# Hybrid block kernel: low-part weight pass moved to the front of each tile, and separate places for low parts

## The chip, the cores and the metric

The kernel runs on one core of a Trainium2 chip. The metric is device time in microseconds (us) of one execution. Before the change the median of three runs is 1329.59 us (1329.51 to 1330.32).

## The reference

Two layers of a hybrid block on 272 tokens (16 meta tokens and 256 of the sequence) of 1024 features. Each layer normalizes, projects the tokens into twelve groups of features, runs three token mixers (retention, HGRN2, differential attention), joins them by gates, projects back, and ends with a gated feed-forward part with a convolution over three tokens. All is float32. Cut to the products with weights, which take nearly all of the time:

```python
proj = (hn @ w_in).astype(F32)
...
y_b = jnp.einsum('blnc,ncd->blnd', branches, w_branch.astype(F32))
...
return y.astype(hn.dtype) @ w_out
...
u = jnp.where(valid[None, :, None], hn @ w_ffn_in, 0.0)
...
return (jax.nn.silu(gate) * val) @ w_ffn_out
```

## The kernel before

**Tiles and passes.** The weights are a stream of 128x128 tiles, 1616 for each layer, in the order in which they are used. A product is computed with features on partitions: a weight tile is the stationary operand, and one 128-feature slice (a "k tile") of the activations, 272 tokens wide, is the moving operand. Each operand is split into a high part, rounded to the float32r format, and a low part, the rest. Three float32r passes go into one PSUM accumulator: high weights with high activations (L868), high weights with low activations (L869), low weights with high activations (L870). Every pass is one LDWEIGHTS and one MATMUL, and TensorE loads the weights of a pass while the pass before still streams. Below, a "step" is the time from the start of one such MATMUL to the start of the next.

**Order.** `ORDER` and `_turns` (L87) list the products in pairs of output tiles. For a pair the order is k = 0 to 7, and for each k the two output tiles (f = 0, 1), so that of two neighbouring tiles every second one moves on to the next k. Only the first two pairs of layer 0 run together: there four tiles share each of the first four k, and every fourth moves on. The feed-forward input is `fi` with 22 pairs (j = 0 to 21) in each layer; its output `fo` has four pairs of 44 tiles in layer 0, and another form in layer 1 (`final`, L1346), where 512 columns of weights stream as the moving operand. In layer 1 most products run on 258 tokens alone (`t0` = `T0` = 14, the first 14 are not needed any more): the moving operand begins 56 bytes later. I call these "short"; the six groups in `FULL` and all of layer 0 have 272 ("full").

**Places of the weights.** Eight tiles arrive in one DMA (`wraw`, 512 KB, a "chunk"). ACT writes their high parts to `whi`, DVE the low parts to `wlo`, four buffers each (`_Weights.next`, L572). `_places` (L125) chooses where in its buffer a tile lies: `APART` and `BLOCK` say at which byte modulo 256 (`LINE`) it is to begin, and 64 is added for each k, as the k tiles of the activations, 1088 bytes long, each begin 64 bytes further modulo 256. High and low part of a tile have the same place. `_runs` (L150) joins tiles whose places follow one rule, so that one ACT and one DVE instruction cut them.

**Distances.** By the addresses in the built program the activations `xh`, `xl` begin at a multiple of 256 bytes and the weight buffers 64 bytes past one; the slots that `b0` to `b2`, `wo` and `fo` use begin at 64 too, which `BLOCK` makes up for. By "distance" I mean the byte address of the weights that are being loaded less that of the operand that streams meanwhile, modulo 256. In full products it is 64 as long as the next pass has the same k, and 128 where the next tile has the next k (L870 streams the high part of k while the high weights of k + 1 are loaded). In short products the two are 104 and 168. The last pair of `fo` in layer 0 has no place asked for (`None`): its tiles lie end to end, and the distance goes through 0, 192, 128 and 64.

**Queues.** All instructions are put in order by a list scheduler (`_Plan.order`) with a modelled cost for each. The cut of a chunk is keyed `LEAD` = 6 us ahead of its first use.

Of the kernel before, what the change touches and what calls it, by code (L numbers as in the profile page):

```python
# [11 lines left out]
F32 = mybir.dt.float32  # L12
F32R = mybir.dt.float32r
U8 = mybir.dt.uint8
AF = mybir.ActivationFunctionType
ALU = mybir.AluOpType
PSUM = bass.MemoryType.PSUM
ADD, SUB, MUL = ALU.add, ALU.subtract, ALU.mult

P = 128  # L20
# [16 lines left out]
CHUNK_TILES = 8  # L37
# [49 lines left out]
def _turns(li):  # L87

    pairs = [x for x in ORDER if x[0][0] not in MARKS]
    if li == DEPTH - 1:
        pairs = [x for x in pairs if x[0] != "fo"]
    groups = [[x] for x in pairs]
    if li == 0:
        groups[:2] = [pairs[:2]]
    turned = [[x] for n in (BASE, ("fi",)) for x in [x for x in pairs if x[0] in n][DEFER - 1 : DEFER]]
    out = []
    for group in groups:  # L100
        if group == [("fo", 3)]:
            out.append([("fo", 3, k, f) for f in range(2) for k in range(FK)])
        else:
            nk = _ktiles(group[0][0])
            out.append([x + (k, f) for k in range(nk // 2) for x in group for f in range(2)])
            out[-1] += [x + (k, f) for x in group for k in range(nk // 2, nk) for f in range(2)]
            if group in turned:
                out[-1] = out[-1][nk:] + out[-1][:nk]
    if li == DEPTH - 1:
        out.append([("fo", j, k, f) for k in range(FK) for j in range(KD // 2) for f in range(2)])  # L110
    return out
# [3 lines left out]


LINE = 256
APART = (0, 96)
BLOCK = 64
ROOM = CHUNK_TILES * P + 2 * LINE // 4  # L120
T0 = META - 2
FULL = ("rk", "rv", "hf", "hi", "dk", "dv")


def _places(depth=DEPTH):  # L125

    wants = []
    for li in range(depth):  # L130
        for name, j, k, _ in sum(_turns(li), []):
            if name == "fo" and (li == DEPTH - 1 or j == 3):
                wants.append(None)
                continue
            short = li == DEPTH - 1 and name not in FULL
            wants.append(APART[short] + BLOCK * (name[0] == "b" or name in ("wo", "fo")) + 64 * (k % 4))
    out = []
    for c in range(0, len(wants), CHUNK_TILES):
        at, places = 0, []
        for want in wants[c : c + CHUNK_TILES]:  # L140
            if want is not None:
                at += (want // 4 - at) % (LINE // 4)
            places.append(at)
            at += P
        assert at <= ROOM
        out.append(places)
    return out


def _runs(places):  # L150


    runs = []
    for i, at in enumerate(places):
        if runs and at == runs[-1][1] + runs[-1][2] * P:
            runs[-1][2] += 1
        else:
            runs.append([i, at, 1])
    out = []
    for i, at, n in runs:  # L160
        if out and out[-1][4] == n and (out[-1][3] == 1 or at == out[-1][1] + out[-1][2] * out[-1][3]):
            if out[-1][3] == 1:
                out[-1][2] = at - out[-1][1]
            out[-1][3] += 1
        else:
            out.append([i, at, 0, 1, n])
    return out


# [388 lines left out]
class _Weights:  # L558
# [6 lines left out]
        self.used = 0  # L565
        self.places = _places()

    def part(self, t, at, step, runs, n):

        return bass.AP(t.tensor, t.offset + at, [list(t.ap[0]), [max(step, 1), runs], [1, n * P]])  # L570

    def next(self):  # L572
        c, i = divmod(self.used, CHUNK_TILES)
        self.used += 1
        if i == 0:
            due = self.plan.key
            room = [P, ROOM]
            raw = self.plan.tile(self.pool, [P, CHUNK_TILES * P], F32, "wraw", 3, f"wraw{c}")
            hi = self.plan.tile(self.pool, room, F32R, "whi", 4, f"whi{c}")
            lo = self.plan.tile(self.pool, room, F32R, "wlo", 4, f"wlo{c}")  # L580
            self.plan.key = due - LEAD
            pieces = 1 if c > 1 else 2
            for p in range(pieces):
                n = CHUNK_TILES // pieces
                cols = slice(p * n * P, (p + 1) * n * P)
                self.sp.dma_start(raw[:, cols], self.w[c][:, cols])
                for first, at, step, runs, each in _runs(self.places[c][p * n : (p + 1) * n]):
                    src = raw[:, (p * n + first) * P : (p * n + first + runs * each) * P].rearrange("p (r x) -> p r x", r=runs)
                    self.act.activation(self.part(hi, at, step, runs, each), src, AF.Copy)
                    self.dve.tensor_tensor(out=self.part(lo, at, step, runs, each), in0=src, in1=self.part(hi, at, step, runs, each).bitcast(F32), op=SUB)  # L590
            self.plan.key = due
            self.cut = hi, lo
        hi, lo = self.cut
        at = self.places[c][i]
        return hi[:, at : at + P], lo[:, at : at + P]

    def chunk(self):

# [13 lines left out]
def _trace(ctx, tc, plan, a, depth, probe):  # L612
    nc = tc.nc
# [79 lines left out]
    inner = masks[:64, 2 * 64 :]  # L693
# [78 lines left out]
    class Norm:  # L772
# [42 lines left out]
        def next(self):  # L815

            self.pairs += 1
            if self.pairs != DEFER + 1:
                return
            self.folded = True  # L820
            ys = []
            for k in range(KD):
                plan.key = clock[0] - 12.0 + 0.3 * k
                if k % 4 == 0:
                    ys.append(slot4("y"))
                y = ys[-1][:, k % 4, :]
                pool.tensor_tensor(out=y, in0=h[:, k, :], in1=rstd, op=MUL)
                plan.key = clock[0] - 6.0 + 0.7 * k
                hi, lo = x_tile(k, True)
                act.activation(hi, y, AF.Identity, scale=self.g[:, k : k + 1])  # L830
                stt(lo, y, self.g[:, k : k + 1], hi.bitcast(F32), MUL, SUB)
# [13 lines left out]
    def products(xs, name, j, t0=0):  # L845

        if name in BASE or name == "fi":
            norm.next()
        if ahead:
            return ahead.pop()  # L850
        tiles = turns.pop(0)
        main = lambda: new(mp, [P, 2, 512], F32, "main", 2, "main")[:, :, t0:T]
        ps = {i: main() for i in sorted({x[1] for x in tiles})}
        to = {x: ps[x[0]][:, x[1], :] for x in {x[1::2] for x in tiles}}
        if (name, j) == ("fo", 3):

            to[j, 1] = main()[:, 1, :]
        cost = 3 * ((T - t0) / 2400 + 0.003)
        left = dict.fromkeys(to, _ktiles(name))
        for _, i, k, f in tiles:  # L860
            hi, lo = (x[:, t0:] for x in xs(k))
            begun = left[i, f] < _ktiles(name)
            left[i, f] -= 1
            plan.key = clock[0]
            wh, wl = weights.next()

            def run(o=to[i, f], wh=wh, wl=wl, hi=hi, lo=lo, first=not begun, last=left[i, f] == 0):
                nc.tensor.matmul(o, wh, hi, start=first, stop=False)  # L868
                nc.tensor.matmul(o, wh, lo, start=False, stop=False)  # L869
                nc.tensor.matmul(o, wl, hi, start=False, stop=last)  # L870

            plan.main.append(plan.add("pe", run, cost, [to[i, f]], [wh, wl, hi, lo]))
            clock[0] += cost
        plan.key = clock[0] - 1.0
        if (name, j) == ("fo", 3):
            return [to[j, f] for f in range(2)]
        ahead.extend(ps[i] for i in ps if i != j)
        return ps[j]
# [64 lines left out]
    for li in range(depth):  # L943
        last = li == depth - 1
# [457 lines left out]
        for name, j in ORDER:  # L1402
# [4 lines left out]
            elif name in ("+hga", "+hgb"):  # L1407
                b = "ab".index(name[3])
# [3 lines left out]
            elif name in ("+daa", "+dab"):  # L1412
                b = "ab".index(name[3])
# [7 lines left out]
            elif name[0] == "*":  # L1421
                plan.key = clock[0] - MARGIN
                n = name[1:]
                if n == "b2":
                    blocks = [st["da0"], st["da1"]]
                else:
                    t = st["rg" if n == "b0" else "hg"]
# [4 lines left out]
            two = slice(2 * (j % 2), 2 * (j % 2) + 2)  # L1432
            both = slice(2 * j, 2 * j + 2)
            if name in BASE:
                lo = 0 if name in FULL else t0
# [17 lines left out]
                elif name in ("dq", "dk"):  # L1453
                    t = block(f"{name}{j // 2}")
# [3 lines left out]
                elif name == "rv":  # L1458
# [3 lines left out]
                    src = values(ps, st["rvt"][j // 2], (j % 2) * 2 * P)  # L1462
# [4 lines left out]
                elif name in ("hi", "dv"):  # L1467
                    n = name[0] + "v"
                    b = j // 2
# [5 lines left out]
                    src = values(ps, st[f"{n}t{b}"], (j % 2) * 2 * P)  # L1475
# [6 lines left out]
                else:  # L1482
                    t = block(f"{name}{j // 2}")
# [21 lines left out]
            elif name == "wo":  # L1505
                hi, lo = st["yhi"], st["ylo"]
# [8 lines left out]
            elif name == "fi":  # L1515
# [8 lines left out]
                first = META if last else 0  # L1524
                c = temp2("two_b")
                for f in range(2):
# [4 lines left out]
                    for back in (1, 2):  # L1531
                        at = max(first, back)
                        stt(c[:, f, at:], u[:, f, at - back - t0 : T - back - t0], w(2 - back), c[:, f, at:], MUL, ADD)
                c = c[:, :, first:]
# [6 lines left out]
            else:  # L1541
                hi, lo = st["ghi"], st["glo"]
# [35 lines left out]
```

## Time and profile before

| | before |
|---|---|
| median of 3 runs | 1329.59 us |
| span of the profiled execution | 1327.6 us |
| TensorE busy (MATMUL) | 1317.0 us, 99% |
| LDWEIGHTS busy | 1288.8 us, 97% |
| DVE busy | 962.7 us, 73% |
| ACT busy | 816.7 us, 62% |
| DMA from HBM | 216.16 MB |

The span is that of one profiled execution from its first to its last instruction; its own time as a run is not listed apart, and the median lies 2.0 us above the span, for what is ahead of the first instruction and behind the last. MATMULs overlap in the records (each has some 290 ns, though one starts every 125 ns), so the busy share says only that TensorE is never without work; what a pass costs is read from the starts. In the timeline a row gives the start in us, the duration in us, the engine, the line, the operation, and output<-input; what stands in brackets is idle time ahead of it and what ended it.

### The profile page before, as it was taken

Reading aid. Unit: us, or ns where it says so; the run is one execution under the profiler, and the core shown is the slowest. Engines: PE = TensorE matmul, PEld = TensorE weight load, DVE = VectorE, ACT = ScalarE, POOL = GpSimd, SP = SyncE. Lnnn points to the kernel's source line nnn. Section 1 sums busy time; section 2 is a strip of 40 time slices with the busy share of each in tenths; the row PEclk is TensorE's granted clock in tenths of the full one; section 3 lists DMA queues with packets and bytes.
Section 4 is the critical chain, followed back from the end, with each engine's and each line's share of the span. In section 5 each row is a group of like instructions: output and inputs, shape, how many; then the busy total and the mean of one; then the engine's idle time right before and its main releaser. Section 6 shows DMA issues by size and latency. Waiting matters only on the chain.

```text
span 1327.6 us, 28926 instructions
## 1 busy us (share of the span) xinstructions
PE 1317.0 (99%) x11862; PEld 1288.8 (97%) x11862; DVE 962.7 (73%) x1630; ACT 816.7 (62%) x1374; POOL 83.6 (6%) x161
## 2 busy tenths in 40 slices
PE   9999999999999999999999999999999999999998
PEld 9999999999999999999999999999999999999986
DVE  7675777697586789886574757776985867898753
ACT  6747454756676567666456474557565775767643
POOL 5000000001010020000030000000011100200000
PEclk9999999999999999999999999999999999999999
DMA  7644543443534545555555445444445446465653
GB/s 272 195 146 155 170 150 128 143 143 129 188 131 158 177 157 176 187 168 186 175 175 181 155 159 161 160 140 143 143 149 175 142 162 199 135 208 189 201 182 109
DMA packets 60755, 219.07 MB, mean 165 GB/s; under 512 B 6864, under 2 KB 6992, under 8 KB 60624
## 3 DMA queue, kind: packets, MB, share of 16 engines
q1 hardware_dynamic: 60336, 216.71, 49.1%
q8 instruction: 93, 1.52, 0.5%
q10 hardware_dynamic: 288, 0.52, 0.1%
q14 instruction: 38, 0.31, 0.1%
HBM read 216.16 MB, written 1.05 MB: 164 GB/s over the span
## 4 chain that ended last, share of the span: by engine, by line
PE 95%; DVE 3%; issue 1%; DMA 0%; ACT 0%; SPq 0%; DVEq 0%
PE main L868 28%; PE main L870 27%; PE main L869 27%; PE fo L1380 2%; PE fo L1378 2%; PE fo L1379 2%; PE lev L1059 1%; DVE two_b L553 1%; PE ds L1243 1%; PE ms L553 1%; PE do L553 1%; DVE wlo L553 1%; PE ro L553 1%; PE ho L553 1%; PE vt L553 1%
## 5 line engine op out<-in xcount | busy, mean ns | idle before, releaser
L868 PE MATMUL main<-xh,whi 128*128 128x272 f32 (+1 forms) x2368 | 693.2, 293 | 0.2 <-ACT whi L553 0.2
L870 PE MATMUL main<-xh,wlo 128*128 128x272 f32 (+1 forms) x2368 | 680.5, 287 | 0.8 <-DVE wlo L553 0.7
L869 PE MATMUL main<-xl,whi 128*128 128x272 f32 (+1 forms) x2368 | 671.6, 284 | 1.6 <-DVE xl L553 1.5
L553 DVE TENSOR_TENSOR wlo<-wraw,whi 128x1024 fp32r<-128x1024 f32 (+1 forms) x408 | 497.1, 1223 | 200.9 <-ACT whi L553 199.8
L553 ACT ACTIVATE whi<-wraw 128x1024 fp32r<-128x1024 f32 (+1 forms) x408 | 426.6, 1048 | 229.5 <-PE main L869 162.2
L869 PEld LDWEIGHTS main<-xl,whi 128*128 128x128 f32 x2368 | 448.9, 190 | 2.5 <-DVE xl L553 2.1
L868 PEld LDWEIGHTS main<-xh,whi 128*128 128x128 f32 x2368 | 445.6, 188 | 2.5 <-issue 0.7
L870 PEld LDWEIGHTS main<-xh,wlo 128*128 128x128 f32 x2368 | 444.6, 188 | 2.2 <-DVE wlo L553 2.1
L553 DVE SCALAR_TENSOR_TENSOR two_b<-main,small,two_b 128x256 f32<-128x256 f32 (+2 forms) x144 | 65.3, 488 | 29.1 <-ACT two_b L553 27.4
L553 POOL TENSOR_TENSOR y<-h,rstd 128x272 f32<-128x272 f32 x32 | 34.6, 1114 | 316.7 <-ACT rstd L553 316.7
L553 ACT ACTIVATE two_b<-main,small 128x272 f32<-128x272 f32 (+1 forms) x72 | 37.3, 567 | 26.8 <-PE main L870 26.6
L870 PE MATMUL main<-ghi,wlo 128*128 128x272 f32 x176 | 51.0, 290 | 0.0
L868 PE MATMUL main<-ghi,whi 128*128 128x272 f32 x176 | 50.9, 289 | 0.0
L869 PE MATMUL main<-glo,whi 128*128 128x272 f32 x176 | 50.2, 285 | 0.0
L553 ACT ACTIVATE vsrc<-main 128x544 f32<-128x544 f32 x24 | 15.0, 626 | 39.4 <-PE main L870 39.2
L868 PE MATMUL main<-b0hi,whi 128*128 128x272 f32 (+1 forms) x128 | 38.1, 298 | 0.0
L868 PE MATMUL main<-b1hi,whi 128*128 128x272 f32 (+1 forms) x128 | 38.1, 298 | 0.0
L870 PE MATMUL main<-yhi,wlo 128*128 128x272 f32 (+1 forms) x128 | 36.7, 286 | 0.0
L870 PE MATMUL main<-b2hi,wlo 128*128 128x272 f32 (+1 forms) x128 | 36.6, 286 | 0.0
L870 PE MATMUL main<-b1hi,wlo 128*128 128x272 f32 (+1 forms) x128 | 36.6, 286 | 0.0
L870 PE MATMUL main<-b0hi,wlo 128*128 128x272 f32 (+1 forms) x128 | 36.6, 286 | 0.0
L868 PE MATMUL main<-yhi,whi 128*128 128x272 f32 (+1 forms) x128 | 36.5, 285 | 0.0
(244 smaller groups left out, 1936.4 us busy)
## 6 DMA issues: line engine op xcount, KB each, us to landing
wraw<-in_w SPq DMA_DIRECT2D x402, 512.0 KB, 3.4
h<-in_h SPq DMA_DIRECT2D x4, 272.0 KB, 5.2
dec<-in_dec SPq DMA_DIRECT2D x2, 544.0 KB, 5.4
wraw<-in_w SPq DMA_DIRECT2D x4, 256.0 KB, 4.6
const<-in_const SPq DMA_DIRECT2D x1, 937.0 KB, 6.1
gain<-in_gl SPq DMA_DIRECT2D x1, 512.0 KB, 6.1
out<-y ACTq DMA_DIRECT2D x2, 256.0 KB, 2.8
out<-y SPq DMA_DIRECT2D x2, 256.0 KB, 2.7
```

Source lines behind the costliest of these rows:

```text
L553: self.plan.add(self.name, lambda: f(*args, **kw), cost, outs, ins, args[2] if method == "activation" else None)
L868: nc.tensor.matmul(o, wh, hi, start=first, stop=False)
L869: nc.tensor.matmul(o, wh, lo, start=False, stop=False)
L870: nc.tensor.matmul(o, wl, hi, start=False, stop=last)
L1059: nc.tensor.matmul(o, keys, x, start=True, stop=True)
L1243: nc.tensor.matmul(ss[m][:, at : at + nk], q[half, hd, q0 : q0 + P], k[half, hd, :nk], start=True, stop=True)
L1378: nc.tensor.matmul(o, gh, wh, start=False, stop=False)
L1379: nc.tensor.matmul(o, gl, wh, start=False, stop=False)
L1380: nc.tensor.matmul(o, gh, wl, start=False, stop=end)
```

## The change

Three things.

1. The three passes of a tile change their order: low weights with high activations, then high with high, then high with low.
2. High and low parts have places of their own. The high part of a tile lies at its distance from the activations of its own k; the low part, which is now loaded while the last pass of the tile before still streams, lies at its distance from the activations of that tile's k (`before`). Distances are counted from the first byte that streams (`moving`, with the 56 bytes of the short products in it). `APART` is 64 for full products, as before, and 160 for short ones, where it was 104 by the same count.
3. The 22 pairs of `fi` get a pair of distances each (high, low), from `SPREAD`, one list for each layer. Only the first entry of each list is that of `APART`.

`_boxes` takes the place of `_runs`: it finds the runs of tiles that one instruction can cut when the raw, the high and the low side each have their own two steps. By the two functions the chunks take 414 cuts on each of ACT and DVE where they took 408.

```diff
-APART = (0, 96)
+BEGIN = 64
...
+APART = (64, 160)
+SPREAD = (
+    [(64, x) for x in (64, 0, 32, 96, 128, 160, 192, 224)]
+    + [(96, x) for x in (64, 32, 96, 128, 0)] + [(144, x) for x in (64, 144, 96)]
+    + [(72, 64), (72, 72), (56, 56), (88, 88), (232, 232), (72, 136)],
+    [(160, x) for x in (160, 0, 32, 64, 96, 128, 192, 224)]
+    + [(x, 160) for x in (104, 80, 208, 168, 152, 232)]
+    + [(104, 104), (104, 40), (168, 168), (80, 80), (80, 16), (208, 208), (104, 232), (176, 160)],
+)
...
-            wants.append(APART[short] + BLOCK * (name[0] == "b" or name in ("wo", "fo")) + 64 * (k % 4))
+            apart = SPREAD[short][j] if name == "fi" else (APART[short],) * 2
+            moving = 4 * T0 * short + BLOCK * (name[0] == "b" or name in ("wo", "fo")) - BEGIN
+            wants.append([x + moving + 64 * (i % 4) for x, i in zip(apart, (k, before))])
+            before = k
...
-                for first, at, step, runs, each in _runs(self.places[c][p * n : (p + 1) * n]):
...
+                mine = [x[p * n : (p + 1) * n] for x in self.places[c]]
+                for first, outer, inner, dims in _boxes(*mine):
+                    src = self.part(raw, (p * n + first) * P, inner * P, P, outer, inner)
+                    to_hi, to_lo = (self.part(t, *x, outer, inner) for t, x in zip((hi, lo), dims))
+                    self.act.activation(to_hi, src, AF.Copy)
+                    self.dve.tensor_tensor(out=to_lo, in0=src, in1=to_hi.bitcast(F32), op=SUB)
...
-        hi, lo = self.cut
-        at = self.places[c][i]
-        return hi[:, at : at + P], lo[:, at : at + P]
+        return tuple(t[:, at[i] : at[i] + P] for t, at in zip(self.cut, self.places[c]))
...
-                nc.tensor.matmul(o, wh, hi, start=first, stop=False)
-                nc.tensor.matmul(o, wh, lo, start=False, stop=False)
-                nc.tensor.matmul(o, wl, hi, start=False, stop=last)
+                nc.tensor.matmul(o, wl, hi, start=first, stop=False)
+                nc.tensor.matmul(o, wh, hi, start=False, stop=False)
+                nc.tensor.matmul(o, wh, lo, start=False, stop=last)
```

More of the change, by code (lines that the diff above doesn't have):

```diff
@@ L130, in _places @@
     for li in range(depth):
+        before = 0
         for name, j, k, _ in sum(_turns(li), []):
@@ L135, in _places @@
             short = li == DEPTH - 1 and name not in FULL
-            wants.append(APART[short] + BLOCK * (name[0] == "b" or name in ("wo", "fo")) + 64 * (k % 4))
+            apart = SPREAD[short][j] if name == "fi" else (APART[short],) * 2
+            moving = 4 * T0 * short + BLOCK * (name[0] == "b" or name in ("wo", "fo")) - BEGIN
+            wants.append([x + moving + 64 * (i % 4) for x, i in zip(apart, (k, before))])
+            before = k
     out = []
     for c in range(0, len(wants), CHUNK_TILES):
-        at, places = 0, []
@@ L140, in _places @@
[L140 to L145, printed above, removed]
+        places = []
+        for part in range(2):
+            at = 0
+            places.append([])
+            for want in wants[c : c + CHUNK_TILES]:
+                if want is not None:
+                    at += (want[part] // 4 - at) % (LINE // 4)
+                places[part].append(at)
+                at += P
+            assert at <= ROOM, at
@@ L146, in _places, with _boxes, box @@
         out.append(places)
     return out
[L150 to L166, printed above, removed]
+def _boxes(*places):
+    def box(first, n):
+        for inner in (n, 2, 1):
+            if n % inner:
+                continue
+            dims = []
+            for at in places:
+                at = at[first : first + n]
+                one = at[1] - at[0] if inner > 1 else P
+                two = at[inner] - at[0] if inner < n else 0
+                if any(at[i] != at[0] + i // inner * two + i % inner * one for i in range(n)):
+                    break
+                dims.append((at[0], two, one))
+            if len(dims) == len(places):
+                return first, n // inner, inner, dims
+        return None
+    out, first, end = [], 0, len(places[0])
+    while first < end:
+        found = next(x for n in range(end - first, 0, -1) if (x := box(first, n)))
+        out.append(found)
+        first += found[1] * found[2]
@@ L566, in __init__, with part @@
         self.places = _places()
-    def part(self, t, at, step, runs, n):
-        return bass.AP(t.tensor, t.offset + at, [list(t.ap[0]), [max(step, 1), runs], [1, n * P]])
+    def part(self, t, at, two, one, outer, inner):
+        return bass.AP(t.tensor, t.offset + at, [list(t.ap[0]), [max(two, 1), outer], [one, inner], [1, P]])
     def next(self):
@@ L586, in next @@
                 self.sp.dma_start(raw[:, cols], self.w[c][:, cols])
-                for first, at, step, runs, each in _runs(self.places[c][p * n : (p + 1) * n]):
-                    src = raw[:, (p * n + first) * P : (p * n + first + runs * each) * P].rearrange("p (r x) -> p r x", r=runs)
-                    self.act.activation(self.part(hi, at, step, runs, each), src, AF.Copy)
-                    self.dve.tensor_tensor(out=self.part(lo, at, step, runs, each), in0=src, in1=self.part(hi, at, step, runs, each).bitcast(F32), op=SUB)
+                mine = [x[p * n : (p + 1) * n] for x in self.places[c]]
[4 more added lines that the diff above has]
+                    self.dve.tensor_tensor(out=to_lo, in0=src, in1=to_hi.bitcast(F32), op=SUB)
             self.plan.key = due
             self.cut = hi, lo
-        hi, lo = self.cut
-        at = self.places[c][i]
-        return hi[:, at : at + P], lo[:, at : at + P]
+        return tuple(t[:, at[i] : at[i] + P] for t, at in zip(self.cut, self.places[c]))
     def chunk(self):
```

## The prediction

> **What bounds the kernel now.** I read the page first: which engine is busy, at what clock, and what the chain that ended last is made of.
>
> ```profile
> span 1327.6 us, 28926 instructions
> PE 1317.0 (99%) x11862; PEld 1288.8 (97%) x11862; DVE 962.7 (73%) x1630; ACT 816.7 (62%) x1374; POOL 83.6 (6%) x161
> PEclk9999999999999999999999999999999999999999
> PE 95%; DVE 3%; issue 1%; DMA 0%; ACT 0%; SPq 0%; DVEq 0%
> PE main L868 28%; PE main L870 27%; PE main L869 27%; PE fo L1380 2%; PE fo L1378 2%; PE fo L1379 2%; PE lev L1059 1%; DVE two_b L553 1%; PE ds L1243 1%; PE ms L553 1%; PE do L553 1%; DVE wlo L553 1%; PE ro L553 1%; PE ho L553 1%; PE vt L553 1%
> ```
>
> 95% of the chain is TensorE, 82% of it the three passes that the change reorders; the clock is full throughout. So the time is the number of passes by the length of a step, and the change leaves the number as it is. Only the step can move. The timeline of TensorE gives it. Three undisturbed stretches: nine pairs of full `fi` (432 steps), eight of short `fi` (384), three of short `b2` (144).
>
> ```profile
> 549.33 0.29 PE L868 MATMUL main<-xh,whi 128*128 128x272 f32 x1
> ...
> 603.21 0.29 PE L868 MATMUL main<-xh,whi 128*128 128x272 f32 x1
> ```
>
> ```profile
> 1201.01 0.28 PE L868 MATMUL main<-xh,whi 128*128 128x258 f32 x1
> ...
> 1246.98 0.28 PE L868 MATMUL main<-xh,whi 128*128 128x258 f32 x1
> ```
>
> ```profile
> 1089.83 0.28 PE L868 MATMUL main<-b2hi,whi 128*128 128x258 f32 x1
> ...
> 1106.83 0.28 PE L868 MATMUL main<-yhi,whi 128*128 128x258 f32 x1
> ```
>
> A full step is 53.88 / 432 = 124.7 ns, a short one 45.97 / 384 = 119.7 ns, and in `b2`, at the same distances, 17.00 / 144 = 118.1 ns. Is that as short as a step can be? The widest passes, 512 columns in the last stage, tell. Nine steps there:
>
> ```profile
> 1280.32 0.39 PE L1378 MATMUL fo<-whi,ghi 128*128 128x512 f32 x1
> ...
> 1282.36 0.40 PE L1378 MATMUL fo<-whi,ghi 128*128 128x512 f32 x1
> ```
>
> 2.04 / 9 = 226.7 ns for 512 columns, 0.443 ns a column: by that rate 272 columns need 120.4 ns and 258 need 114.2. So a full step carries 4.3 ns and a short one 5.5 ns that streaming doesn't explain. Over 5904 full steps (5772 of them with places) and 3264 short ones that is 25 + 18 us, all that any placement could give. Does the place matter at all? The last `fo` pair of layer 0 has tiles end to end, at four distances in turn; its first 66 steps:
>
> ```profile
> 658.57 0.29 PE L868 MATMUL main<-ghi,whi 128*128 128x272 f32 x1
> ...
> 666.89 0.29 PE L868 MATMUL main<-ghi,whi 128*128 128x272 f32 x1
> ```
>
> 8.32 / 66 = 126.1 ns, 1.4 more than at 64 with every sixth load at 128. A quarter of these are at 64 (as good as below, 123.7), so the other three average 126.9. The effect is real and small.
>
> **The change part by part.** *Full products outside `fi`: 1572 tiles, 4716 steps.* The weights' order becomes low, high, high; still two loads under a high and one under a low activation, and the distances in a tile stay 64. What goes is the one load in six at 128, when k moves on. Its worth shows in the first two pairs of layer 0, where only every fourth tile moves on, so one load in twelve is at 128. 24 steps there:
>
> ```profile
> 8.13 0.29 PE L868 MATMUL main<-xh,whi 128*128 128x272 f32 x1
> ...
> 11.11 0.29 PE L868 MATMUL main<-xh,whi 128*128 128x272 f32 x1
> ```
>
> 2.98 / 24 = 124.2 ns (the rows' rounding leaves 123.8 to 124.6). Halving the shifted loads took 0.5 ns off 124.7; taking the other half too gives 123.7 (122.9 to 124.5). 4716 x 1.0 ns = 4.7 us gained, between 0.9 and 8.5.
>
> [...]
>
> *Short products outside `fi`: 736 tiles, 2208 steps.* Distance 160 for all loads, in place of 104 and 168. No row of before has 160, and the weights now begin 24 bytes past a multiple of 64, where they were at 32. Below, the step cannot beat the 114.2 of streaming; above, the bad three quarters of the `fo` pair are 2.2 ns worse than 124.7, so 121.9. At one place the trace has 119.7 and 118.1. I take 119.0, 0.7 less than now, because the mixture goes here as in the full products, and no more, because the new place is unknown: -1.5 us, between -12.1 and +4.9.
>
> *`fi` of layer 0: 1056 steps.* One pair has (64, 64); the others leave 64 for one of three loads (low part elsewhere) or for all. Nearest is the `fo` pair again: between 123.7 as for realigned and 126.9. I take 125.4, between them: +0.7 us, bounds -1.1 to +2.3.
>
> *`fi` of layer 1: 1056 steps.* The 119.0 of above with the same loss of some 0.7 for scatter gives 119.7: nothing, bounds -5.8 to +2.3.
>
> *Low part first.* The first pass of a chunk now waits for DVE's `wlo`, which comes after ACT's `whi`. Where the cut is early that costs nothing; it is late here:
>
> ```profile
> 500.00:510.00 10.00, 9.55 (x74) 9.12 (x74) 10.00 (x20) 7.04 (x13) 0.00 (x0) 1.00 0.45 157
> 1140.00:1160.00 20.00, 18.50 (x157) 18.29 (x156) 19.93 (x34) 15.13 (x27) 7.62 (x7) 1.00 0.35 116
> ```
>
> ```profile
> 6.79 0.39 PE L870 MATMUL main<-xh,wlo 128*128 128x272 f32 x1 [0.21 <-DVE wlo L553]
> ...
> 13.49 0.39 PE L870 MATMUL main<-xh,wlo 128*128 128x272 f32 x1 [0.21 <-DVE wlo L553]
> ...
> 507.31 0.39 PE L870 MATMUL main<-xh,wlo 128*128 128x272 f32 x1 [0.32 <-DVE wlo L553]
> ```
>
> In the two stretches of the windows view (columns: length, then TensorE, loads, DVE, ACT, POOL busy, clock, DMA) DVE is busy all the time and TensorE waits: DVE sets the pace early in both `fi` stages, and at the very start. Such a wait stood ahead of the third pass, with two passes done; now it stands ahead of the first, and all three are queued behind it, 2 x 0.125 us = 0.25 us later. What waits for them is the pair's accumulator and then ACT and DVE, who have the next chunks to cut. In a stretch paced by DVE only the last wait counts. Four such places: +1.0 us, between +0.5 and +2.5 if every late chunk pays.
>
> *Cuts.* Six more each on ACT and DVE. The page has the cut's mean:
>
> ```profile
> L553 DVE TENSOR_TENSOR wlo<-wraw,whi 128x1024 fp32r<-128x1024 f32 (+1 forms) x408 | 497.1, 1223 | 200.9 <-ACT whi L553 199.8
> L553 ACT ACTIVATE whi<-wraw 128x1024 fp32r<-128x1024 f32 (+1 forms) x408 | 426.6, 1048 | 229.5 <-PE main L869 162.2
> ```
>
> The elements stay the same, so only the fixed part of six instructions is added, a fraction of 1.2 us each and under 2 us of DVE in all, hidden by 200 us in which DVE waits ahead of its cuts; uncovered it would cost those 2 us at the start. The patterns get one more dimension; were a cut 5% slower (25 us of DVE over the run), only the DVE-paced 30 us would show it, some 1 us. I count nothing. DMAs, SP's queue and the passes' number are untouched, and the 132 steps of the last `fo` pair and the last stage keep their places.
>
> *Sum.* -4.7 - 1.5 + 0.7 + 0 + 1.0 = -4.5 us. The span of 1327.6 becomes 1323.1; with the 2.0 us that the median lies above it, 1325.1.
>
> **The rivals.** *Placement gives nothing (20%).* [...] For it: one 24-step stretch with its rounding carries my largest term. Against it: the `fo` pair. What is left is the +1.0 of waits: 1330.6, and 1329.6 without these.
>
> *Short products at 160 are worse (24%), the slower side.* [...] At the 2.2 ns of the bad `fo` distances it costs 3264 x 2.2 = 7.2 us, and scattered `fi` pairs of layer 0 another 1.5 (1056 x 1.4). With -4.7 and +1.0: +5.0, 1334.6. It decides from about 1.7 ns a short step, where it has eaten the rest and 0.2% besides (3264 x 1.7 = 5.5 against -4.7 + 0.7 + 1.0). For it: the weights begin at no multiple of 16 bytes any more, and 160 is near 168, whose loads the change itself treats as misplaced. Against it: `b2` ran at 118.1 with 168 in the mixture.
>
> *Short products find a clean place (14%).* At 116 ns, between 118.1 and the 114.2 of streaming, 2208 x 3.7 = 8.2 us, and `fi` at 117.5 another 2.3; with -4.7, +0.7 and +1.0: -13.5, 1316.1. [...]
>
> **How the numbers follow.** The forecast, realignment pays a little and the rest about cancels, has 42%: 1325.1, its own range 1321 to 1328.5 (the bounds 0.9 and 8.5 of the first term). 0.2%, 2.7 us, is about what a measurement of this kernel can tell from no change. Faster by more than that: 36 of the forecast's 42, and the 14 of the clean place: 50%. Within: 6 of the forecast, and the 20 of no effect: 26%. Slower: 24%. The range of 8 in 10 goes from 1317.5, into the clean place, to 1334, into the bad one.
>
> **What would show it.** Full pairs outside `fi`: 48 steps in 5.94 us (123.7) prove the first term, 5.99 disprove it. Short pairs: 5.71 us (119.0) as forecast, over 5.8 the slower rival, under 5.6 the clean place. The 22 pairs of `fi` should scatter, and within layer 0 no pair should pass 127 ns a step. Waits for `wlo` should stand ahead of the first pass at the same few chunks. The prediction is wrong if short steps move by over 2 ns, or if the full ones stay at 124.7.

## The result, and the profile after

| | before | after |
|---|---|---|
| median of 12 runs | 1329.51 us | 1328.51 us |
| ratio to before | | 0.9991 (95% interval 0.9983 to 0.9999) |
| span of the profiled execution | 1327.6 us | 1326.9 us |

About 1 us less: the sign of the forecast, inside its range, but a quarter of the 4.5 us that it named, and less than the 0.2% that I had called telling. The medians below leave out one run of e1, of 1591.83 us at a granted clock of 0.752. The page of the changed kernel, the lines that answer to those quoted of before:

```profile
span 1326.9 us, 28961 instructions
PE 1314.5 (99%) x11862; PEld 1285.8 (97%) x11862; DVE 962.8 (73%) x1636; ACT 817.5 (62%) x1380; POOL 85.2 (6%) x161
PE 94%; DVE 3%; issue 1%; ACT 1%; DMA 0%; POOL 0%; SPq 0%; DVEq 0%; POOLq 0%
L892 PE MATMUL main<-xh,wlo 128*128 128x272 f32 (+1 forms) x2368 | 692.8, 293 | 4.4 <-DVE wlo L577 4.4
L577 DVE TENSOR_TENSOR wlo<-wraw,whi 128x1024 fp32r<-128x1024 f32 (+1 forms) x414 | 497.6, 1208 | 204.3 <-ACT whi L577 201.9
```

The same 11862 passes, six more cuts, and TensorE still is the chain. Its first pass (L892, the low weights) now idles 4.4 us behind DVE. The rest is in the steps. From the timeline of TensorE, first steps of pairs in full products outside `fi`: 48 steps lie between the first two rows, 192 between the last two.

```profile
27.02 0.29 PE L892 MATMUL main<-xh,wlo 128*128 128x272 f32 x1
33.06 0.29 PE L892 MATMUL main<-xh,wlo 128*128 128x272 f32 x1
...
45.05 0.28 PE L892 MATMUL main<-xh,wlo 128*128 128x272 f32 x1
...
68.78 0.28 PE L892 MATMUL main<-xh,wlo 128*128 128x272 f32 x1
```

6.04 / 48 = 125.8 ns and 23.73 / 192 = 123.6 ns: the same kind of product, at the same distances, at two paces. I call a pair undisturbed if each of its steps is under 140 ns. Before, the 47 undisturbed full pairs all had 124.5 to 124.7. In the changed kernel 28 full pairs outside `fi` are undisturbed: 20 at 123.6 to 123.8 and 8 at 125.7 to 125.9, the one pace or the other and nothing between. The single steps, from the differences of the starts in the trace in ns, six to a line (two tiles):

```
slow (hf, second pair)     fast (hg, first pair)
131 120 125 127 122 124    121 125 127 122 124 123
129 125 128 126 127 126    121 125 126 123 124 122
131 120 125 127 122 124    121 125 127 122 125 122
129 125 128 126 127 126    121 125 127 122 124 123
```

Both repeat exactly, the slow one every 12 steps, the fast one every 18, and from the last pair of `hf` to `hi` each pair hands its cycle on to the next. In short products (192 steps of `hg` in layer 1, which `hi` with 272 columns follows) the pace is 22.67 / 192 = 118.1 ns, where it was 119.7:

```profile
711.54 0.28 PE L892 MATMUL main<-xh,wlo 128*128 128x258 f32 x1
...
734.21 0.29 PE L892 MATMUL main<-xh,wlo 128*128 128x272 f32 x1
```

The same 192 steps before, 22.99 us:

```profile
711.54 0.28 PE L868 MATMUL main<-xh,whi 128*128 128x258 f32 x1
...
734.53 0.29 PE L868 MATMUL main<-xh,whi 128*128 128x272 f32 x1
```

Put together, with the mean of all steps under 140 ns (longer ones have other work between) by kind of product, from the starts in the two traces:

| steps | before, ns | after, ns | difference | forecast |
|---|---|---|---|---|
| full outside `fi`, 4716 | 124.56 | 124.32 | -1.1 us | -4.7 us |
| short outside `fi`, 2208 | 119.26 | 118.55 | -1.6 us | -1.5 us |
| `fi` of layer 0, 1056 | 124.69 | 125.13 | +0.5 us | +0.7 us |
| `fi` of layer 1, 1056 | 119.48 | 119.05 | -0.5 us | 0 |
| TensorE's waits | 4.1 us in all | 6.2 us in all | +2.1 us | +1.0 us |

The sum is -0.6 us, and the span fell by 0.7. In the views of what TensorE waited for (us in total, times, the longest), the rows of the weights' and activations' low parts, first before and then after:

```profile
PE main L869 <- DVE xl L553: 1.5, 1, 1.5
PE main L870 <- DVE wlo L553: 0.7, 3, 0.3
```

```profile
PE main L892 <- DVE wlo L577: 4.4, 7, 1.2
PE main L894 <- DVE xl L577: 0.2, 1, 0.2
```

### The profile page after: what moved, and what is told of

Its sections match the earlier page's. It is cut to its first block, busy times and chain, and to the rows that moved or that the text cites. A ratio compares the mean times of both kernels' runs of the same rounds, so it can differ in the third digit from the quotient of the medians.

```text
span 1326.9 us, 28961 instructions
## 1 busy us (share of the span) xinstructions
PE 1314.5 (99%) x11862; PEld 1285.8 (97%) x11862; DVE 962.8 (73%) x1636; ACT 817.5 (62%) x1380; POOL 85.2 (6%) x161
## 4 chain that ended last, share of the span: by engine, by line
PE 94%; DVE 3%; issue 1%; ACT 1%; DMA 0%; POOL 0%; SPq 0%; DVEq 0%; POOLq 0%
PE main L892 27%; PE main L893 27%; PE main L894 27%; PE fo L1402 2%; PE fo L1404 2%; PE fo L1403 2%; PE lev L1083 1%; DVE two_b L577 1%; PE ds L1267 1%; PE ms L577 1%; PE do L577 1%; PE ro L577 1%; DVE wlo L577 1%; PE ho L577 1%; PE vt L577 1%
## 5 line engine op out<-in xcount | busy, mean ns | idle before, releaser
L892 PE MATMUL main<-xh,wlo 128*128 128x272 f32 (+1 forms) x2368 | 692.8, 293 | 4.4 <-DVE wlo L577 4.4
L893 PE MATMUL main<-xh,whi 128*128 128x272 f32 (+1 forms) x2368 | 676.1, 286 | 0.0
L577 DVE TENSOR_TENSOR wlo<-wraw,whi 128x1024 fp32r<-128x1024 f32 (+1 forms) x414 | 497.6, 1208 | 204.3 <-ACT whi L577 201.9
L892 PEld LDWEIGHTS main<-xh,wlo 128*128 128x128 f32 x2368 | 447.3, 189 | 7.9 <-DVE wlo L577 3.1
L892 PE MATMUL main<-ghi,wlo 128*128 128x272 f32 x176 | 50.7, 288 | 0.0
L892 PE MATMUL main<-b0hi,wlo 128*128 128x272 f32 (+1 forms) x128 | 38.1, 297 | 0.0
L892 PE MATMUL main<-b1hi,wlo 128*128 128x272 f32 (+1 forms) x128 | 38.0, 297 | 0.0
L577 POOL COPY tails<-vsrc 128x32 f32<-128x32 f32 x32 | 10.9, 355 | 421.1 <-ACT vsrc L577 421.1
L893 PE MATMUL main<-b2hi,whi 128*128 128x272 f32 (+1 forms) x128 | 36.5, 285 | 0.0
```

The source lines that it names most:

```text
L577: self.plan.add(self.name, lambda: f(*args, **kw), cost, outs, ins, args[2] if method == "activation" else None)
L892: nc.tensor.matmul(o, wl, hi, start=first, stop=False)
L893: nc.tensor.matmul(o, wh, hi, start=False, stop=False)
```

## Experiments

The theory that I formed from this trace: with all loads at distance 64 a full step has two stable cycles, and the nanoseconds of the last interruption choose between them. Rival: the pace of a pair is set by what runs beside TensorE (ACT and DVE writing the same memory, DMA), which is the program's and not chance.

**e1: no scatter.** All pairs of `fi` at the distances of `APART`.

```diff
-            apart = SPREAD[short][j] if name == "fi" else (APART[short],) * 2
+            apart = (APART[short],) * 2
```

> The changed kernel without the list of distances: all 44 pairs of fi at (64, 64) or (160, 160). Theory (a full step with all loads at 64 has two cycles, 123.6 and 125.8 ns, and keeps the one that the last interruption set): each undisturbed fi pair of layer 0 is at 123.6 or at 125.8 and nothing between; layer 1 at 117.7 to 118.3 (119.0 on the mean in the changed kernel). 1326 to 1328.5 us. Rival (what runs beside TensorE sets the pace of a pair): fi pairs take values of their own, as the scattered ones did.

1327.65 us (median of ten runs), ratio 0.9984 (0.9975 to 0.9993). The ten fall into two heaps, five at 1326.2 to 1326.9 and five at 1328.4 to 1329.6 us. The traced one, of 1328.37 us, is of the upper heap. In it, of 46 undisturbed full pairs 20 were at 123.6 to 123.7, 25 at 125.7 to 125.9, and one at 123.9. In `fi` of layer 0 all 720 steps from the eighth pair to the end were slow. From the timeline of e1, the ends of that stretch, and then of the 132 steps of each of three pairs of `fo`:

```profile
518.48 0.29 PE L892 MATMUL main<-xh,wlo 128*128 128x272 f32 x1
...
609.08 0.29 PE L892 MATMUL main<-ghi,wlo 128*128 128x272 f32 x1
...
625.68 0.29 PE L892 MATMUL main<-ghi,wlo 128*128 128x272 f32 x1
...
642.01 0.29 PE L892 MATMUL main<-ghi,wlo 128*128 128x272 f32 x1
...
658.61 0.29 PE L892 MATMUL main<-ghi,wlo 128*128 128x272 f32 x1
```

90.60 / 720 = 125.8 ns; then 16.60, 16.33 and 16.60 us, slow, fast, slow. Had all 1056 steps of `fi` in layer 0 been fast, that would be worth some 2.3 us (an estimate, 1056 x 2.2 ns), about what parts the two heaps of times; no run of the lower heap was traced, so this stays a guess. So the scatter of the changed kernel was no loss in layer 0 against this trace: its 22 pairs had 125.1 on the mean, the unscattered ones here 125.8. In layer 1 the unscattered ones had 118.1 against 119.05, 1 us better.

**e2: the order of passes alone.** Low and high part at the places of before.

```diff
-APART = (64, 160)
+APART = (64, 104)
...
-            wants.append([x + moving + 64 * (i % 4) for x, i in zip(apart, (k, before))])
+            wants.append([x + moving + 64 * (i % 4) for x, i in zip(apart, (k, k))])
```

(and the line of e1.)

> The new order of passes alone, low and high part at the places of before (64 and 104, one load in six shifted by 64). If the gain comes from the places: full steps all at 124.7 again in one cycle, short at 119.7 or 118.1, and the time is that of before plus the waits for the low part, 1330 to 1331.5 us. If the order itself helps: below 1329 us.

1330.65 us, ratio 1.0007 (0.9998 to 1.0015): all 46 undisturbed full pairs at 124.5 to 124.7 again, short ones at 118.0 to 119.9, as before. The order by itself moves no step. What it adds are the waits: TensorE waited 3.9 us for `wlo` and 0.2 for `xl`, where before it had been 0.7 and 1.5; all its waits came to 5.7 us against 4.1.

**e3: realigned, but short products still at 104.** As e1 with `APART = (64, 104)`.

> As e1, with short products at 104 in place of 160. By the pair (104, 104) of the changed kernel, 121.4 ns a step: 3264 x (121.4 - 118.2) = 10 us more than e1, some 1337 us. Rival, that realignment and not the distance brought the gain of the short products: 118 to 119 ns, within 2 us of e1.

1332.38 us, ratio 1.002 (1.0011 to 1.0029): 4.7 us more than e1, where I had expected 10, and more in every run than in any of e1's ten. Short steps had 120.4 outside `fi` and 120.2 in it, most undisturbed pairs at 119.8 to 120.1 or at 121.4. So in short products realignment alone is a loss (119.3 before, 120.4 now), and the new distance is the gain (118.5). Layer 0 of this kernel has the instructions and addresses of e1, one for one; they differ from the first chunk of layer 1 on. Its timeline, the same stretch of 720 steps:

```profile
518.61 0.28 PE L892 MATMUL main<-xh,wlo 128*128 128x272 f32 x1
...
607.61 0.29 PE L892 MATMUL main<-ghi,wlo 128*128 128x272 f32 x1
```

89.00 / 720 = 123.6 ns. One program, one stage, two paces: the stage entered the one cycle in e1 and the other in e3, and that alone was worth 1.6 us. In `fi` the two part in the seventh pair (125.7 and 123.6), behind the waits for DVE.

**e4: one shifted load at the head of each full pair.**

```diff
+            if (name, j) not in pairs and not short and len(wants) > 32:
+                wants[-1][1] += 64
             before = k
+            pairs.add((name, j))
```

> As e1, with the low part of the first tile of each full pair 64 bytes further (one load of 48 at distance 128). Theory: that one shifted load sets the phase anew at each pair, so all undisturbed full pairs run in the same cycle: at 123.6 to 123.8 (3 us less than e1) or all at 125.8 (some 6 us more). Rival, that what runs beside TensorE sets the pace: the same pairs as in e1 are slow and fast, and the time is that of e1 plus 0.3 us.

1327.12 us, ratio 0.998 (0.9971 to 0.9989). Neither all fast nor all slow. From its timeline, the heads of five pairs of `fi` in a row:

```profile
542.81 0.29 PE L895 MATMUL main<-xh,wlo 128*128 128x272 f32 x1
...
548.75 0.29 PE L895 MATMUL main<-xh,wlo 128*128 128x272 f32 x1
...
554.79 0.29 PE L895 MATMUL main<-xh,wlo 128*128 128x272 f32 x1
...
560.73 0.29 PE L895 MATMUL main<-xh,wlo 128*128 128x272 f32 x1
...
566.77 0.29 PE L895 MATMUL main<-xh,wlo 128*128 128x272 f32 x1
```

5.94, 6.04, 5.94, 6.04 us: 123.8 and 125.8 in turn, through 16 pairs. My expectation that the shift sets the phase anew was wrong: it exchanges the two cycles. For the rival it is the end: in e1 and e3 these pairs, with the same work beside them, kept one pace each, slow in e1 and fast in e3, and alternate only with the shifted load.

**e5: other distances.** From the scattered pairs of the changed kernel I took the best: (96, 32), and (160, 128) for short products. Their rows, from the timeline of the changed kernel, the pair at (96, 64) and then the one at (96, 32):

```profile
525.13 0.29 PE L892 MATMUL main<-xh,wlo 128*128 128x272 f32 x1
...
531.20 0.28 PE L892 MATMUL main<-xh,wlo 128*128 128x272 f32 x1
...
537.14 0.29 PE L892 MATMUL main<-xh,wlo 128*128 128x272 f32 x1
```

6.07 and 5.94 us: 126.3 and 123.8 ns by the starts in the trace, from another place of the low part alone.

```diff
+            apart = (64, 64) if name == "fo" else ((96, 32), (160, 128))[short]
```

(`fo` stays, because its tiles would not fit into `ROOM`.)

> As e1, with full products but fo at (96, 32) and short ones at (160, 128). In the changed kernel the pair of fi at (96, 32) ran at 123.8 ns and that at (160, 128) at 117.3. If these places have one cycle alone: all undisturbed full pairs within 0.1 of 123.8, short ones at 117.3; 4716 x 0.45 + 1056 x 2.0 + 3264 x 1.0 ns = 7.5 us less than e1, 1321 us. If they have two cycles as (64, 64) has: two heaps, and a time within 3 us of e1.

1324.05 us, ratio 0.9958 (0.9946 to 0.9971). Every run lies below the fastest of e1. Of 46 undisturbed full pairs 42 were at 123.6 to 123.8, two at 124.1, and the two at 125.7 and 125.8 are `fo` with its old places. From its timeline, the 720 steps of `fi` in layer 0, and 672 in layer 1:

```profile
518.46 0.29 PE L892 MATMUL main<-xh,wlo 128*128 128x272 f32 x1
...
607.46 0.29 PE L892 MATMUL main<-ghi,wlo 128*128 128x272 f32 x1
...
1168.66 0.28 PE L892 MATMUL main<-xh,wlo 128*128 128x258 f32 x1
...
1247.25 0.28 PE L892 MATMUL main<-xh,wlo 128*128 128x258 f32 x1
```

89.00 / 720 = 123.6 and 78.59 / 672 = 116.9 ns. No slow heap of full pairs is left where the places changed; of 32 short ones two sat at 121.3 and 121.4, so a second pace is left there. The gain over e1 is 3.6 us, not the 7.5 expected: full products outside `fi` have 124.20 on the mean, little under e1's 124.26, because their disturbed pairs did not improve. Over all these products the first twelve steps behind one of 140 ns or more have 124.9 on the mean and the later ones 123.8 (e1: 124.3 and 124.2). This kernel beats both of the case.

**e6: (72, 64) and (168, 160).** As e5 with these.

> As e1, with full products at (72, 64), short ones at (168, 160); these pairs of fi ran at 124.0 and 117.75 ns in the changed kernel. One cycle alone: all undisturbed full pairs at 124.0, short ones at 117.8, some 3 us less than e1. Two cycles: two heaps.

1328.77 us, ratio 0.9991 (0.9982 to 1.0001). Full pairs sat at 125.2 to 125.6, 44 of 46 undisturbed ones; the 124.0 of the single pair in the changed kernel was not its settled pace. Short ones stood mostly at 117.5, near the 117.8 expected. A pair of 48 steps behind other distances is too short a probe.

**e7: several shifts at the head of a pair.** As e1; in layer 0 the shift goes by groups.

```diff
+KINDS = (
+    (("hf", (1, 2, 3)), 0, -64), (("hg", (0, 1, 2, 3)), 0, 32), (("b2", (0, 1, 2, 3)), 0, -32),
+    (("wo", (0, 1, 2, 3)), 64, 0), (("fi", (0, 1, 2, 3)), 0, 0), (("fi", (6, 7, 8, 9)), -64, 0), (("fi", (10, 11, 12, 13)), 0, 8),
+    (("fi", (14, 15, 16, 17)), 0, 16), (("fi", (18, 19, 20, 21)), 32, 0),
+)
...
+                wants[-1][0] += kind[0]
+                wants[-1][1] += kind[1]
```

> As e1, where in layer 0 groups of four pairs have one shift each at their first tile: low part by -64, +32, -32, +8, +16, high part by +64, -64, +32, and one group none. Theory (a shift at the head of a pair maps one cycle to the other, as +64 of the low part did in e4): in each group the pairs alternate (the shift flips), stay at 123.6 (it leads to the fast cycle from both) or stay at 125.8, and the group without a shift keeps what it entered with. Rival (what runs beside sets the pace): no pattern by group.

One run, 1327.8 us. Low +32, +8 or +16, high +64: the pairs alternate (at low +8 6.03, 5.94, 6.02 and 5.94 us, 125.6, 123.8, 125.4 and 123.8 ns by the starts). No shift: they keep the slow cycle in which they entered, 125.8. High +32: all four slow, 125.8, though a fast pair stood ahead. High -64: all four fast, 123.9, as the pair ahead. Low -32: slow, as the pair ahead, then three fast. Low -64: both undisturbed pairs slow. A pattern by group, as the theory had it, but for the slow first pair of low -32: it follows a product whose activations begin at another address modulo 256, so its first load lies at distance 96, where the other three have 32. Its timeline, four pairs with high -64 (23.79 us for 192 steps), then two with low +8, and at the end four with high +32:

```profile
512.77 0.28 PE L905 MATMUL main<-xh,wlo 128*128 128x272 f32 x1
...
536.56 0.29 PE L905 MATMUL main<-xh,wlo 128*128 128x272 f32 x1
...
542.59 0.29 PE L905 MATMUL main<-xh,wlo 128*128 128x272 f32 x1
...
548.53 0.29 PE L905 MATMUL main<-xh,wlo 128*128 128x272 f32 x1
...
584.41 0.28 PE L905 MATMUL main<-xh,wlo 128*128 128x272 f32 x1
...
608.57 0.29 PE L905 MATMUL main<-ghi,wlo 128*128 128x272 f32 x1
```

**e8: e1 once more.**

> The kernel of e1 once more. If the last interruption sets the cycle, its nanoseconds decide, and they differ from run to run: undisturbed stretches are again at 123.6 or 125.8 and nothing between, but not all in the same one as in e1. Rival (set by the program): every pair as in e1.

One run, 1328.74 us, and mostly the pairs of e1: both paces, `fi` of layer 0 slow again. But the last pair of `m2` in layer 0 was slow (125.9) where e1 had 123.7, and the three pairs of `fo` stood the other way round, from its timeline:

```profile
609.78 0.29 PE L892 MATMUL main<-ghi,wlo 128*128 128x272 f32 x1
...
626.10 0.29 PE L892 MATMUL main<-ghi,wlo 128*128 128x272 f32 x1
...
642.70 0.29 PE L892 MATMUL main<-ghi,wlo 128*128 128x272 f32 x1
...
659.03 0.29 PE L892 MATMUL main<-ghi,wlo 128*128 128x272 f32 x1
```

16.32, 16.60, 16.33 us: fast, slow, fast, where e1 had slow, fast, slow. The same instructions fell into the other cycle. That the nanoseconds of interruptions decide it is argued, not shown: no run sets them. The three pairs of `fo` count as one such event, because their cycle changes at both borders between them in the changed kernel, e1, e3, e5, e7, e8 and e9 alike, though no load is displaced there. Why it does, when pairs of `fi` hand theirs on, stays open.

**e9: e5 with the cut keyed earlier.** `LEAD = 8.0`.

> As e5, with the cut of a chunk keyed 8 us ahead of its first use in place of 6. In e5 TensorE waits 4.1 us for the low part, 3.3 more than in the third pass of before. If the waits come from DVE, which is busy without a break early in both fi stages, an earlier key cannot help: 3.5 to 4.5 us of waits, 1324 us. Rival, that the cut is merely keyed too late for a part that is needed first: the waits fall to about 1 us, 1321 us.

1323.55 us, ratio 0.9958 (0.9944 to 0.9972): the time of e5. What TensorE waited for, in us, times, and the longest:

```profile
PE main L894 <- DVE xl L577: 3.3, 4, 1.5
PE warm L577 <- POOL ones_d L577: 1.0, 1, 1.0
PE main L892 <- DVE wlo L577: 0.9, 2, 0.7
```

The waits for the low weights fell to 0.9 us, as the rival had it, and 3.3 us of waits for `xl`, the low part of the activations, came in their place (0.2 in e5). DVE was late in all, whichever of its products was put first: 4.2 us of waits for `wlo` and `xl` here, 4.3 in e5 (4.1 and 0.2). The time is DVE's, as the theory had it, though not by waits on `wlo`.

## Why the prediction was right, and where it was wrong

*Full products outside `fi`, -4.7 us forecast, -1.1 measured: the step that failed.* I read 124.2 ns off 24 steps with half the shifted loads and drew the line on to 123.7 for none. The pace is there, 123.6 to the tenth, but in 20 of the 28 undisturbed pairs; the other eight sit at 125.8, above the 124.7 of before. A mean pace was treated as a function of the mean distance. e1, e3, e4 and e8 show that it is a cycle, which one displaced load exchanged (e4: 123.8 and 125.8 ns in turn) and which the same instructions did not always enter alike (`fi` of layer 0: 125.8 in e1, 123.6 in e3). That is the smaller part of what is missing, about 1 us of 3.6. The larger, some 2.3 us, is that I gave the gain to all steps, while of the 4397 under 140 ns 2753 stand in pairs that were disturbed before: these went from 124.49 to 124.34 alone, and with e5's places, where settled pairs are fast, they still have 124.31. Why they miss the settled pace stays open; e5's slow first dozen steps behind an interruption is all that the runs show of it. The rest, 0.3 us, is 319 steps over 140 ns. The warning was in the profile: `b2` and `fi` in layer 1 at 118.1 and 119.7 with equal distances. I had both numbers and did not carry their difference into the term. The regular shift of before was a load at 128 every sixth step; with it only one full pace was seen (124.5 to 124.7 in all 47 undisturbed pairs, and again in e2).

*Short products, -1.5 forecast, -1.6 measured: right in size by luck, wrong in its reason.* I had taken 0.7 ns for the realignment and nothing for the place. e3 shows the realignment at 104 costing 1.1 ns a step, and 160 in place of it paying 1.9. The slower rival, 160 worse than 104, is refuted.

*`fi`*, forecast +0.7 and 0, measured +0.5 and -0.5: within bounds, for both; no scattered full pair passed 126.4.

*Waits*, forecast +1.0, measured +2.1 in the trace (and +1 us of time in e2, its interval from -0.3 to +2): the late places were the expected ones, at the start and early in both `fi`, but a wait grew by more than two passes (0.25 us) where DVE's cut, 1.2 us long, had long to go. Nearly all of it came at the start (0.6 us before, 2.3 after) and once in `fi` of layer 0; early in `fi` of layer 1 the waits are 1.5 us in both kernels, for `xl` before and mostly for `wlo` now. The first of all and the one in `fi` of layer 0, from the timeline of the changed kernel:

```profile
6.37 0.40 PE L892 MATMUL main<-xh,wlo 128*128 128x272 f32 x1 [1.21 <-DVE wlo L577]
...
506.82 0.36 PE L892 MATMUL main<-xh,wlo 128*128 128x272 f32 x1 [0.77 <-DVE wlo L577]
```

Before, 0.32 us stood at the second place, and at the first 0.17:

```profile
6.06 0.40 PE L868 MATMUL main<-xh,whi 128*128 128x272 f32 x1 [0.17 <-ACT whi L553]
```

In the changed kernel DVE was busy 10.00 of the 10 us from 500 to 510 and 19.93 of the 20 from 1140 to 1160, as before, and e9, with its 4.2 us of waits for DVE at an earlier key, bears out that DVE paces these stretches. *Cuts* hidden, as forecast: 414 of them, 1208 ns each, 497.6 us in all against 497.1.

*That placement gives nothing* is refuted by e5, where against e1, with the same passes, addresses alone took 3.6 us off. In the changed kernel the pairs at (96, 64) and (96, 32) differ by 2.5 ns a step. What inside the chip makes the difference no run shows.

The total of 1328.5 stayed in the range although 3.6 us of the first term were missing and 1.1 us of waits came on top; what I had called the likeliest case was not what happened, and the measured 0.1% belongs to the case of no telling change. That it landed inside is luck, the more so as e1's two heaps lie 2.4 us apart, more than twice the change measured.

## What to carry to other kernels

Where one engine is full for a whole kernel (here TensorE, 99% of the span), look at the few ns in each instruction before the waits: 2.2 ns in each of the 1056 steps of `fi` in layer 0 would be 2.3 us (an estimate), where the longest wait of the changed kernel for the weights was 1.2 us. They depended on addresses here (126.3 ns at (96, 64), 123.8 at (96, 32)); but judge a place by whether all undisturbed stretches settle at its pace (a histogram by stretch), not by a mean or by one short stretch: in e6 one pair had promised 124.0, and 44 of 46 settled at 125.2 to 125.6. One displaced load moved the steps into the other cycle (e4: 123.8 and 125.8 ns in turn). Without one a cycle lasted 90.6 us in e1, and one stage entered either in two runs, 125.8 ns in e1 and 123.6 in e3, 2% apart with the same instructions and addresses in the stage. The pace of settled stretches said little of those that are interrupted again and again: in e5 42 of 46 settled full pairs were at 123.6 to 123.8, and the pairs outside `fi` that were disturbed before had 124.31. Moving the operand that is produced last to the front of each unit cost its producer's slack (all waits of TensorE 4.1 us before, 5.7 in e2), and an earlier key didn't buy it back where that producer was full (4.3 us of waits for DVE in e5, 4.2 in e9).

## What the hardware showed that I had not expected

- Two self-repeating sequences of steps at equal instructions, distances and granted clock (123.6 and 125.8 ns for 272 columns at (64, 64), a granted clock of 0.999 in e1 and e3), handed on across pairs of `fi` and exchanged between pairs of `fo` (16.60, 16.33 and 16.60 us in e1); one load 64 bytes off (e4), or 16 or even 8 (e7), exchanged them. At (96, 32) the undisturbed pairs of e5 stood at 123.6 to 124.1, most at 123.6.
- Short products had several paces too: 116.9 and 121.3 at (160, 128) in e5, 117.5 at (168, 160) in e6, 117.7 to 118.6 at (160, 160) in the changed kernel, 119.8 to 121.5 at (104, 104) in e3.
- 512 columns took 226.7 ns before, 0.443 ns a column, and no cycle came to that rate with 272 (120.4). What inside the chip makes the cycles, and why only one was seen at (96, 32), stays open; no run here looks inside.
